# Moving a bias table forward, joining value products, and moving half of a modulation: a two-block transformer kernel on one core

## The chip, the cores and the metric

The kernel runs on 1 core of one Trainium2 chip. The metric is the device time of one execution in microseconds (us); the median of 3 runs before the change is 2052.93 us (2050.81 to 2061.72). Names of engines: PE is the matmul engine, PEld its weight loads, DVE the vector engine, ACT the scalar engine, POOL the GpSimd engine, SP the engine that issues most loads. ACTq and SPq are DMA issues by ACT and by SP.

## The reference, cut to what matters

Two transformer blocks run one after the other on 512 tokens of width 1024, in float32. The first block mixes by two kinds of attention with a relative-position bias, then has a SwiGLU feed-forward. The second block has two layers whose normed input is scaled and shifted by vectors ("modulation") computed from one conditioning vector `c`:

```python
# first block
xn = rms_norm(h, norm1_g); aq, ak, av, ... = split_columns(xn @ w_in)
o_a = mixer_dilated(aq, ak, av, rel_bias[:, :8])     # 8 heads, bias of the distance
o_b = gates over compressed, selected and window attention (8 heads, rel_bias[:, 8:])
h = h + concat(o_a, o_b) @ w_out
h = h + (silu(hn @ w_gate) * (hn @ w_up)) @ w_down   # hn = rms_norm(h), 2816 hidden
x = rms_norm(h, norm_f_g)
# second block, layers i = 0 (gated linear attention + attention), 1 (window attention)
mod_l = split(silu(c) @ mod_w[i] + mod_b[i], 6)      # mod_w[i]: 1024 x 6144
h_l = rms_norm_2(x, norm_mix[i]) * (1 + mod_l[1]) + mod_l[0]
x = x + mod_l[2] * mixer(h_l);  x = x + mod_l[5] * hier_moe(modulated x)
```

`mod_w[i]` does not depend on the tokens, so the modulation vectors of both layers can be computed at any time ahead of their use. Layer 1's are first needed in layer 1, at the end of layer 0's expert part.

## The kernel before, in words

**Arithmetic.** Every float32 product is made of three matmuls of split operands (high times high, low times high, high times low): lines L155, L156, L157. A weight tile of 128x1024 (512 KB, one load by SP) is cast to its high half on ACT (`whi`, L149) and subtracted for its low half on DVE (`wlo`, L150). In `even_layer`, `proj_T` takes POOL for that subtraction when three projections share one pass (`eng=nc.gpsimd`).

**Order.** A scheduler puts all instructions in one order per engine when the program is built, and each engine runs its list in that order, waiting on semaphores. DMAs are issued by an engine's queue, so they stand in these lists too.

**Bias table.** `first_block` makes a table of biases. After the value projection `w_av`, `bias_rows()` loads three small tables by ACT, multiplies them (L302), finishes them on DVE (L303), stores the result `bd` (16x640) and copies every row of it 128 times to a table `bf` of [16, 128, 640] in memory (5.24 MB): four DMAs of 1280 KB each, issued by ACT. `bias_tile` later loads, for each head and half of the queries, one tile `wb` of 128 rows out of `bf`, each row one element further on: 32 loads by SP (L131). DVE subtracts `wb` from the scores (L384).

**Attention.** Scores go through a softmax on DVE and ACT (`sc`), four PE transposes (`tr`, L199), an eviction to `pt`, and the value products `po` (L404 in the first block, L2166 in the last layer; values `av`, `bvn`, `avN`, `ovN`). `Fill` hands PE work from the head before while a head's scores are made: one call between two groups of scores issues `n` items, here FILL0, FILL1 and FILLA = 1.

**Modulation.** `mod_steps` (L692) is a generator; one step loads 128 rows of `mod_w` (512 KB, SP) for 1024 of the columns and adds `row * silu(c)` to a 128x1024 accumulator `macc` by two DVE instructions (L709 for the first, L711 for the rest). After eight steps PE sums the partitions (L718), and the row is added to `modrow` (L721). 16 steps and a tail make one third (`rd`), three thirds a layer. Layer 0's 48 steps are spread over the first block's feed-forward by `next(steps, None)`. Layer 1's 48 steps are spread over `even_layer`, one after each projection piece and after each output of the linear attention; what is left is done before `m_es.close()`.

**Operand of layer 0.** `cross_norm` (L960 to L971) norms the feed-forward's result; `modulated_T` transposes it (L199 `tr<-ident,X`), scales it on ACT to `ms` (L769), and DVE makes the halves `ahi`, `alo` (L771, L772). Then come the projections of layer 0, the gates `gG` of the linear attention, its scans (L1096, L1098), states and outputs (`gat` L1161, `go` L1165, `sr` L1172).

Of the kernel before, what the change touches and what calls it, by code (L numbers as in the profile page):

```python
# [19 lines left out]
P = 128  # L20
# [44 lines left out]
FILL0 = 1  # L65
FILL1 = 1
# [5 lines left out]
FILLA = 1  # L72
# [143 lines left out]
def first_block(K, st, h_es):  # L216

    tc, nc, io, small = K.tc, K.nc, K.io, K.small
    es = ExitStack()
    g1 = K.c.tile([P, KT], F32, name="g1")  # L220
# [8 lines left out]
    def acc():  # L229
        return ps_a.tile([P, 512], F32, name="acc", tag="acc", bufs=2)  # L230

    xn = K.act_lat()
    with ExitStack() as w_es:
        work = K.pool(w_es, "b1w")
        x = work.tile([P, NT, D], F32, name="x")
        for t in range(NT):
            K.load(x[:, t], io["x"][t * P:(t + 1) * P])
        for p in range(2):
            xs = []
            for t in (2 * p, 2 * p + 1):  # L240
                junk = work.tile([P, D], BF16, name="junk", tag="junk", bufs=2)
                r = K.rsqrt(K.sumsq(x[:, t], junk), D)
                nc.vector.tensor_scalar(x[:, t], x[:, t], r, None, op0=OP.mult)
                xs.append(x[:, t])
            normed_T(K, ps_t, xs, 2, g1, lambda k: (xn[0][:, k, 256 * p:256 * p + 256], xn[1][:, k, 256 * p:256 * p + 256]))

# [42 lines left out]


    bd = K.dram.tile([16, 640], F32, name="bd")
    bf = K.dram.tile([16, P, 640], F32, name="bf")

    def bias_rows():
        t1, t2, bv = [att.tile([P, 1024], F32, name="bt", tag="pt", bufs=4) for _ in range(3)]
        relb, oneh, brow, bv = t1[:32, 640:656], t1[:32, :640], t2[:16, :640], bv[:16, :640]
        K.store(relb, io["rel_bias"])
        K.store(oneh, io["c_onehot"])
        K.store(brow, io["c_brow"])
        for s0, w in ((0, 512), (512, 128)):  # L300
            ps = acc()
            nc.tensor.matmul(ps[:16, :w], relb, oneh[:, s0:s0 + w], start=True, stop=True)  # L302
            nc.vector.scalar_tensor_tensor(bv[:, s0:s0 + w], ps[:16, :w], -1.0, brow[:, s0:s0 + w],  # L303
                                           op0=OP.mult, op1=OP.subtract)
        K.store(bd, bv)
        for h in range(0, 16, 4):
            K.store(bf[h:h + 4], bd[h:h + 4, None, :].to_broadcast([4, P, 640]))
# [212 lines left out]
    bias_rows()  # L520
# [73 lines left out]
    steps = mod_steps(K, st, 0, st["pool"], ps_t)  # L594
    def ff_up(f):
        pss = []
        for i, src in enumerate((io["w_gate"], io["w_up"])):
# [9 lines left out]
            next(steps, None)  # L607
# [20 lines left out]
    for f in range(22):  # L628
        ff_up(f)
        if f == CTX_AT:  # L630
            for _ in steps:
                pass
# [7 lines left out]
        if f == parts[0][1]:  # L640

            f0, f1 = parts.pop(0)
            for ch in range(2):
                chunks = load(f0, f1, ch)
                for t in range(NT):
# [3 lines left out]
                    if t:  # L649
                        next(steps, None)  # L650
# [19 lines left out]
    for t in range(NT):  # L670
# [7 lines left out]
        if t % 2:  # L678
            modulated_T(K, work, ps_t, xs, gs, cols, 0, h, P * (t - 1))
# [12 lines left out]
def mod_steps(K, st, l, pool, psum):  # L692
# [4 lines left out]
    for rd in range(3):  # L697
# [190 lines left out]
class Fill:  # L888


    def __init__(self, n):
        self.n, self.todo = n, iter(())

    def __call__(self):
        for _ in range(self.n):
# [80 lines left out]
def even_layer(K, st, h, rt):  # L976
# [20 lines left out]
    steps = mod_steps(K, st, 1, modp, ps_t)  # L997
# [4 lines left out]
    def proj_T(parts, *pairs):  # L1002
        ws = [K.weights(io["ev_s"][i], eng=nc.gpsimd if len(pairs) == 3 else None) for i, _ in pairs]
        for sl in parts:
            for w, (_, evac) in zip(ws, pairs):
# [4 lines left out]
                next(steps, None)  # L1010

    def proj_N(src, width, evac, parts=((4, 5, 0, 1, 2, 3),)):
        chunks = [K.weights(src[kp]) for kp in range(KT * width // D)]
        for ts in parts:
            for t in ts:
# [3 lines left out]
                next(steps, None)  # L1019
# [129 lines left out]
    def outputs(j):  # L1149
        ss = small.tile([P, CH, 2], F32, name="gss", tag="gss", bufs=2)  # L1150
        s4 = sr.rearrange("p c (h d) -> p c h d", h=4)
        for ch in (4, 5, 1, 2, 0, 3):
            cs = slice(ch * P, (ch + 1) * P)
            for e in range(2):
# [18 lines left out]
                next(steps, None)  # L1173
# [1188 lines left out]
def body(nc, tc, io, out, stop=None, skip1=False, force_slow=False):  # L2362
    with ExitStack() as es:
# [9 lines left out]
        if skip1:  # L2373
# [3 lines left out]
            with ExitStack() as mes:  # L2377
# [9 lines left out]
                for p in range(3):  # L2387
# [5 lines left out]
                    modulated_T(K, work, pt, xs, gs, cols, p // 2, h, 256 * p)  # L2393
# [86 lines left out]
```

## Time and profile before

| what | value |
|---|---|
| median of 3 runs (lowest, highest) | 2052.93 us (2050.81, 2061.72) |
| profiled execution, its own time | 2055.75 us |
| its span | 2054.0 us |
| PE busy | 1814.8 us, 88% of the span |
| DVE busy | 1456.9 us, 71% |
| ACT busy | 934.6 us, 46% |
| POOL busy | 421.2 us, 21% |
| mean granted clock of PE | 0.934 |
| DMA moved | 314.80 MB, mean 153 GB/s |

The span is the time from the first to the last instruction of the profiled execution; its own time is 1.75 us longer, and 2.82 us above the median of the runs. Busy time is an average over stages with different limits. A timeline row gives the start in us, the duration in us, engine, line, operation, output and inputs and, in brackets, how long the engine was idle before it and what it waited for. A row of a table by stretch gives the stretch, its length, the busy time of PE, PEld, DVE, ACT and POOL in it (instructions in parentheses), the granted clock as a share of the full one, the busy share of the DMA engines and the GB/s moved.

### The profile page before, as it was taken

What the parts mean: (1) busy time and instruction counts of PE and PEld (TensorE: products, weight loads), DVE (VectorE), ACT (ScalarE), POOL (GpSimd) and SP (SyncE); (2) the same over time, 40 slices, a digit from 0 to 9 for tenths busy, and PEclk for the clock granted to TensorE, in tenths of its full rate; (3) what the DMA queues carried; (4) which work ended last, traced back from release to release, by engine and by line L of the source; (5) the groups of instructions that cost most, each with busy time, mean ns of one, the idle gap of its engine ahead of it and who ended that gap; (6) DMA issues with size and microseconds to landing.
All of it is one profiled execution on the core that took longest, in us unless ns stands there. A gap on an engine that the chain in (4) does not pass through costs nothing. (4 is left out here: it accounts for less than half of the span.)

```text
span 2054.0 us, 27111 instructions
## 1 busy us (share of the span) xinstructions
PE 1814.8 (88%) x9494; PEld 1368.3 (67%) x9494; DVE 1456.9 (71%) x2809; ACT 934.6 (46%) x1777; POOL 421.2 (21%) x330
## 2 busy tenths in 40 slices
PE   7499999899999996898978998599957899978997
PEld 5377865777777775676756677476746666765664
DVE  4264676697676448667867635799979877568999
ACT  4264465422222233421325732378844467426673
POOL 0010011100000011030222122333234411144752
PEclk9799999999999997897989999699978999988998
DMA  6333221475655225454430144489852100548983
GB/s 220 137 100 104 83 62 52 138 242 167 199 174 173 81 88 161 144 157 160 154 101 1 42 176 154 170 313 348 304 201 85 42 1 12 200 157 275 329 288 137
DMA packets 99662, 314.80 MB, mean 153 GB/s; under 512 B 15904, under 2 KB 19617, under 8 KB 99505
## 3 DMA queue, kind: packets, MB, share of 16 engines
q1 hardware_dynamic: 77856, 267.97, 39.3%
q10 hardware_dynamic: 13168, 23.91, 3.1%
q0 software_dynamic: 8480, 20.98, 3.0%
q8 instruction: 78, 1.28, 0.3%
q14 instruction: 80, 0.65, 0.1%
HBM read 291.18 MB, written 36.32 MB: 159 GB/s over the span
## 5 line engine op out<-in xcount | busy, mean ns | idle before, releaser
L149 ACT CAST whi<-wraw 128x1024 fp32r<-128x1024 f32 (+1 forms) x345 | 359.1, 1045 | 417.7 <-PE acc L156 134.3
L150 DVE TENSOR_TENSOR wlo<-wraw,whi 128x1024 fp32r<-128x1024 f32 (+1 forms) x337 | 400.9, 1214 | 93.2 <-ACT whi L149 89.8
L711 DVE SCALAR_TENSOR_TENSOR macc<-wraw,silu,macc 128x1024 f32<-128x1024 f32 x168 | 214.8, 1317 | 12.7 <-DMA wraw<-mod_w 12.7
L155 PE MATMUL acc<-ahi,whi 128*128 128x512 f32 (+1 forms) x576 | 215.5, 375 | 3.6 <-ACT whi L149 1.7
L157 PE MATMUL acc<-ahi,wlo 128*128 128x512 f32 (+1 forms) x576 | 215.0, 374 | 3.7 <-DVE wlo L150 3.7
L156 PE MATMUL acc<-alo,whi 128*128 128x512 f32 (+1 forms) x576 | 215.1, 374 | 0.0
L199 PE MATMUL tr<-ident,sc 128*128 128x128 f32 x752 | 128.8, 287 | 2.2 <-DVE alo L213 0.7
L155 PEld LDWEIGHTS acc<-ahi,whi 128*128 128x128 f32 x576 | 109.4, 190 | 26.3 <-ACT fhi L161 2.5
L157 PEld LDWEIGHTS acc<-ahi,wlo 128*128 128x128 f32 x576 | 109.8, 191 | 22.4 <-DVE wlo L150 4.1
L199 PEld LDWEIGHTS tr<-ident,sc 128*128 128x128 f32 x752 | 82.0, 141 | 63.3 <-issue 34.3
L156 PEld LDWEIGHTS acc<-alo,whi 128*128 128x128 f32 x576 | 109.7, 190 | 18.7 <-issue 0.4
L156 PE MATMUL gu<-wlo,xhi 128*128 128x512 f32 (+1 forms) x264 | 110.1, 417 | 12.1 <-DVE wlo L150 10.8
L155 PE MATMUL acc<-whi,ahi 128*128 128x512 f32 (+2 forms) x288 | 105.9, 372 | 8.1 <-DVEq L1227 8.1
L157 PE MATMUL gu<-whi,xlo 128*128 128x512 f32 (+1 forms) x264 | 106.0, 401 | 2.7 <-DVE xlo L161 2.6
L155 PE MATMUL gu<-whi,xhi 128*128 128x512 f32 (+1 forms) x264 | 106.9, 405 | 0.9 <-ACT xhi L161 0.8
L157 PE MATMUL acc<-whi,alo 128*128 128x512 f32 (+2 forms) x288 | 104.8, 368 | 1.0 <-DVE alo L772 1.0
L156 PE MATMUL acc<-wlo,ahi 128*128 128x512 f32 (+2 forms) x288 | 104.7, 366 | 0.8 <-DVE wlo L150 0.8
L1733 POOL DMA_INDIRECT xg<-hD,xidx x33 | 72.5, 2197 | 149.2 <-PE yo L157 64.4
L928 POOL COPY rw<-rd 128x256 f32<-128x256 f32 x52 | 21.5, 413 | 363.0 <-DVE rd L934 165.5
L1743 POOL DMA_INDIRECT yD<-y,idx x33 | 73.1, 2217 | 87.8 <-DVE y L1813 29.1
L962 POOL TENSOR_TENSOR xs<-X,gf 128x1024 f32<-128x1024 f32 x2 | 5.8, 2922 | 367.5 <-DVE X L622 367.5
L884 PE MATMUL sps<-Kh,Q 128*128 128x256 f32 (+2 forms) x208 | 73.6, 361 | 7.1 <-DVE mn L2140 5.5
(548 smaller groups left out, 4402.9 us busy)
## 6 DMA issues: line engine op xcount, KB each, us to landing
wraw<-ew SPq DMA_DIRECT2D x198, 512.0 KB
wraw<-mod_w SPq DMA_DIRECT2D x96, 512.0 KB
wraw<-w_gate SPq DMA_DIRECT2D x22, 512.0 KB
wraw<-w_up SPq DMA_DIRECT2D x22, 512.0 KB
wraw<-w_down SPq DMA_DIRECT2D x22, 512.0 KB
wraw<-yD SPq DMA_DIRECT2D x20, 512.0 KB
wraw<-w_s SPq DMA_DIRECT2D x16, 512.0 KB
wraw<-w_out SPq DMA_DIRECT2D x12, 512.0 KB
```

What stands on the lines that cost most here:

```text
L149: nc.scalar.copy(hi[:, :n], raw[:, :n])
L150: (eng or nc.vector).tensor_tensor(lo[:, :n], raw[:, :n], hi[:, :n].bitcast(F32), op=OP.subtract)
L155: mm(out, a[0], b[0], start=start, stop=False)
L156: mm(out, a[0], b[1], start=False, stop=False)
L157: mm(out, a[1], b[0], start=False, stop=stop)
L199: self.nc.tensor.transpose(out, src, self.ident[:n, :n])
L711: nc.vector.scalar_tensor_tensor(acc[:, r], w, sr, acc[:, r], op0=OP.mult, op1=OP.add)
L884: K.nc.tensor.matmul(ps, q, Kh[:, cols], start=True, stop=False)
L928: K.nc.gpsimd.tensor_copy(rw, r[:, :, :, None].to_broadcast([P, 2, 2, 64]))
L962: (V if late else nc.gpsimd).tensor_tensor(y, x, gf, op=OP.mult)
L1733: return nc.gpsimd.indirect_dma_start(out=xg[:c], out_offset=None, in_=mo["hD"], bounds_check=n * P - 1, oob_is_err=False, in_offset=bass. ...
L1743: sc = nc.gpsimd.indirect_dma_start(out=yD.rearrange("t k d -> (t k) d"), out_offset=bass.IndirectOffsetOnAxis(ap=idx[:c, b:b + 1].bitcast ...
```

## The change

Four things change.

- The three small tables are loaded first of all by ACT, the two matmuls and two DVE instructions on them stand at the program's start, and `bd` and `bf` are written by POOL's queue behind the norm of `x`. `bf` has 32 copies of each row instead of 128 (1.31 MB, two DMAs), and each `wb` tile is loaded in four DMAs of 32 rows.
- `Fill` issues on every second call only, three items instead of one (FILL0, FILL1), or two (FILLA).
- `mod_steps` takes the thirds to do. Layer 1's first third follows layer 0's steps in the feed-forward's calls, what is left of it is done behind the loop, and its two other thirds stay in `even_layer`, each step ordered behind the last instruction of layer 0's operand (`tc.issue_after`).
- `proj_T` of `even_layer` always subtracts on DVE.

```diff
-FILL0 = 1
-FILL1 = 1
+FILL0 = 3
+FILL1 = 3
-FILLA = 1
+FILLA = 2
...
+    K.store(relb, io["rel_bias"])
+    K.store(oneh, io["c_onehot"])
+    K.store(brow, io["c_brow"])
     g1 = K.c.tile([P, KT], F32, name="g1")
...
+    bf = K.dram.tile([16, 32, 640], F32, name="bf")
+    for s0, w in ((0, 512), (512, 128)):
+        ps = acc()
+        nc.tensor.matmul(ps[:16, :w], relb, oneh[:, s0:s0 + w], start=True, stop=True)
+        nc.vector.scalar_tensor_tensor(bv[:, s0:s0 + w], ps[:16, :w], -1.0, brow[:, s0:s0 + w],
+                                       op0=OP.mult, op1=OP.subtract)
...
+    nc.gpsimd.dma_start(bd, bv)
+    for h in range(0, 16, 8):
+        nc.gpsimd.dma_start(bf[h:h + 8], bd[h:h + 8, None, :].to_broadcast([8, 32, 640]))
...
-        K.store(bd, bv)
-        for h in range(0, 16, 4):
-            K.store(bf[h:h + 4], bd[h:h + 4, None, :].to_broadcast([4, P, 640]))
...
-        src = bass.AP(tensor=bf.tensor, offset=bf.offset + h * P * 640 + 127 + (2 - 2 * p) * P, ap=[[639, P], [1, n]])
-        K.load(w[:, :n], src)
+        for r in range(0, P, 32):
+            src = bass.AP(tensor=bf.tensor, offset=bf.offset + h * 32 * 640 + 127 + (2 - 2 * p) * P - r, ap=[[639, 32], [1, n]])
+            K.load(w[r:r + 32, :n], src)
...
     proj_N(io["w_av"], 512, lambda t, ps: nc.any.tensor_copy(av[:, t], ps))
-    bias_rows()
...
-    steps = mod_steps(K, st, 0, st["pool"], ps_t)
+    mods = [mod_steps(K, st, 0, st["pool"], ps_t), mod_steps(K, st, 1, st["pool"], ps_t, (0,))]
+
+    def step():
+        while mods and next(mods[0], 1):
+            mods.pop(0)
...
+    while mods:
+        step()
     m_es.close()
...
         if t % 2:
-            modulated_T(K, work, ps_t, xs, gs, cols, 0, h, P * (t - 1))
+            st["mark"] = modulated_T(K, work, ps_t, xs, gs, cols, 0, h, P * (t - 1)).ins
...
-        for _ in range(self.n):
+        self.calls += 1
+        for _ in range(0 if self.calls % 2 else self.n):
             next(self.todo, None)
...
-    steps = mod_steps(K, st, 1, modp, ps_t)
+    steps = mod_steps(K, st, 1, modp, ps_t, (1, 2))
+
+    def step():
+
+        with tc.issue_after(st["mark"]):
+            next(steps, None)
...
-        ws = [K.weights(io["ev_s"][i], eng=nc.gpsimd if len(pairs) == 3 else None) for i, _ in pairs]
+        ws = [K.weights(io["ev_s"][i]) for i, _ in pairs]
```

What the scheduler makes of it is seen at three places. A row is a number, the line, the operation, output and inputs, the output's size and, with x, how many stand in a row; lines of the changed kernel are those of its own file.

DVE at the program's start, before:

```order
7 L180 TENSOR_SCALAR ss<-ss 128x1
8 L243 TENSOR_SCALAR x<-x,rs 128x1024
9 L180 TENSOR_SCALAR ss<-ss 128x1
10 L243 TENSOR_SCALAR x<-x,rs 128x1024
11 L213 SCALAR_TENSOR_TENSOR alo<-tr,g_83,ahi 128x256 x2
12 L150 TENSOR_TENSOR wlo<-wraw,whi 128x1024 x2
```

and now:

```order
5 L245 SCALAR_TENSOR_TENSOR bv<-acc,brow 16x512
6 L245 SCALAR_TENSOR_TENSOR bv<-acc,brow 16x128
7 L180 TENSOR_SCALAR ss<-ss 128x1 x4
8 L150 TENSOR_TENSOR wlo<-wraw,whi 128x1024 x3
9 L259 TENSOR_SCALAR x<-x,rs 128x1024 x4
10 L213 SCALAR_TENSOR_TENSOR alo<-tr,g_93,ahi 128x256 x2
```

The bias rows `bv` and three low halves of `w_av` now stand ahead of the scaling of `x`.

PE in the last layer's attention, before:

```order
6803 L2166 MATMUL po<-pt,ovN 64x256 x2
6804 L199 MATMUL tr<-ident,sc 128x128 x5
6805 L884 MATMUL sps<-Kh,Q 128x256
6806 L885 MATMUL sps<-Kl,Q 128x256
6807 L884 MATMUL sps<-Kh,Q 128x256
6808 L885 MATMUL sps<-Kl,Q 128x256
6809 L2166 MATMUL po<-pt,ovN 64x256 x2
```

and now:

```order
6758 L199 MATMUL tr<-ident,sc 128x128 x4
6759 L893 MATMUL sps<-Kh,Q 128x384
6760 L894 MATMUL sps<-Kl,Q 128x384
6761 L893 MATMUL sps<-Kh,Q 128x256
6762 L894 MATMUL sps<-Kl,Q 128x256
6763 L2182 MATMUL po<-pt,ovN 64x256 x4
6764 L2182 MATMUL po<-pt,ovN 64x128 x2
```

The same 416 value products of the four attentions stand in 106 uninterrupted runs instead of 199 (`av` 18 instead of 21, `bvn` 28 instead of 47, `avN` 25 instead of 53, `ovN` 35 instead of 78).

DVE behind the operand of layer 0, before:

```order
743 L711 SCALAR_TENSOR_TENSOR macc<-wraw,silu,macc 128x1024
744 L772 TENSOR_TENSOR alo<-ms,ahi 128x256
745 L771 CAST ahi<-ms 128x256
746 L711 SCALAR_TENSOR_TENSOR macc<-wraw,silu,macc 128x1024
747 L772 TENSOR_TENSOR alo<-ms,ahi 128x256
748 L771 CAST ahi<-ms 128x256
```

and now:

```order
748 L781 TENSOR_TENSOR alo<-ms,ahi 128x256
749 L804 TENSOR_TENSOR evqc<-cos,evqg 128x256
750 L805 TENSOR_TENSOR evqs<-sin,evqg 128x256
751 L804 TENSOR_TENSOR evkc<-cos,evkg 128x256
752 L805 TENSOR_TENSOR evks<-sin,evkg 128x256
753 L718 TENSOR_SCALAR macc<-wraw,silu 128x1024 x2
754 L720 SCALAR_TENSOR_TENSOR macc<-wraw,silu,macc 128x1024 x14
755 L150 TENSOR_TENSOR wlo<-wraw,whi 128x1024 x3
756 L730 TENSOR_TENSOR modrow<-modrow,tr 64x512
757 L718 TENSOR_SCALAR macc<-wraw,silu 128x1024 x2
758 L720 SCALAR_TENSOR_TENSOR macc<-wraw,silu,macc 128x1024
759 L1103 COPY gkT<-acc 128x256
```

The steps of the modulation no longer stand between the halves of the operand but in one block behind them, ahead of the gates, which begin two rows further on.

## Rows read from the trace of the kernel before

**Rows 1.** Busy time by stretch (columns as said above).

```profile
50.00:100.00 50.00, 21.18 (x82) 16.92 (x80) 9.10 (x11) 7.65 (x12) 0.00 (x0) 0.69 0.38 138
...
105.00:361.00 256.00, 247.19 (x1426) 180.44 (x1425) 159.53 (x445) 142.12 (x355) 26.16 (x48) 1.00 0.27 78
...
650.00:750.00 100.00, 100.00 (x443) 79.63 (x442) 38.51 (x57) 26.95 (x35) 0.00 (x0) 1.00 0.27 81
...
850.00:926.00 76.00, 76.00 (x351) 57.71 (x350) 51.45 (x65) 25.45 (x44) 15.95 (x15) 0.98 0.44 145
...
967.00:1047.00 80.00, 71.11 (x465) 56.82 (x465) 66.35 (x99) 27.24 (x79) 16.66 (x12) 0.91 0.51 158
...
1640.00:1810.00 170.00, 163.12 (x1054) 117.25 (x1052) 115.81 (x290) 100.05 (x255) 29.65 (x42) 0.97 0.21 80
```

**Rows 2.** Timeline of PE around its long gap.

```profile
56.48 0.39 PE L157 MATMUL acc<-ahi,wlo 128*128 128x512 f32 x1
84.63 0.47 PE L884 MATMUL sps<-akh,aq 128*128 128x128 f32 x1 [27.76 <-ACT akh L878]
86.16 0.77 PE L155 MATMUL acc<-ahi,whi 128*128 128x512 f32 x1 [1.06 <-DVE aq L867]
...
91.84 0.53 PE L156 MATMUL acc<-alo,whi 128*128 128x512 f32 x1
```

**Rows 3.** Timeline of ACT's queue in the same stretch.

```profile
50.09 32.79 ACTq L134 DMA_DIRECT2D bf<-bd  x4
```

**Rows 4.** Four microseconds in which only the table is written (columns of rows 1).

```profile
74.00:78.00 4.00, 0.00 (x0) 0.00 (x0) 0.00 (x0) 0.00 (x0) 0.00 (x0) 0.50 0.26 104
```

**Rows 5.** Timeline at the start, of ACT and of PE.

```profile
17.95 1.98 ACT L149 CAST whi<-wraw 128x1024 fp32r<-128x1024 f32 x2
...
16.33 0.78 PE L155 MATMUL acc<-whi,ahi 128*128 128x512 f32 x1
```

**Rows 6.** Timeline of SP: two loads of bias tiles back to back.

```profile
104.12 0.80 SPq L131 DMA_DIRECT2D wb<-bf  x2
```

**Rows 7.** Timeline of PE: value products in runs of 4 and of 14.

```profile
1704.10 0.65 PE L2166 MATMUL po<-pt,ovN 128*64 128x256 f32 x4
1704.68 0.77 PE L199 MATMUL tr<-ident,sc 128*128 128x128 f32 x5
...
1705.64 0.28 PE L885 MATMUL sps<-Kl,Q 128*128 128x256 f32 x1
1705.85 0.65 PE L2166 MATMUL po<-pt,ovN 128*64 128x256 f32 x4
...
164.28 1.73 PE L404 MATMUL po<-pt,av 128*64 128x256 f32 x14
165.94 0.44 PE L199 MATMUL po<-ident,rw 128*128 128x128 f32 x2
```

**Rows 8.** Timeline of DVE and of POOL from the operand of layer 0 to the gates.

```profile
763.62 0.75 DVE L970 TENSOR_SCALAR X<-xs,rs 128x1024 f32<-128x1024 f32 x1 [2.90 <-POOL rs L185]
...
778.89 2.83 DVE L970 TENSOR_SCALAR X<-xs,rs 128x1024 f32<-128x1024 f32 x1 [0.59 <-POOL rs L185]
...
782.84 1.27 DVE L711 SCALAR_TENSOR_TENSOR macc<-wraw,silu,macc 128x1024 f32<-128x1024 f32 x1
...
808.00 0.42 DVE L772 TENSOR_TENSOR alo<-ms,ahi 128x256 fp32r<-128x256 f32 x1
...
836.85 0.48 DVE L1064 TENSOR_SCALAR gG<-acc,gb 128x256 f32<-128x256 f32 x1
...
778.83 2.34 POOL L150 TENSOR_TENSOR wlo<-wraw,whi 128x1024 fp32r<-128x1024 f32 x1
```

**Rows 9.** Timeline of DVE at the second scan of the linear attention.

```profile
972.84 9.65 DVE L711 SCALAR_TENSOR_TENSOR macc<-wraw,silu,macc 128x1024 f32<-128x1024 f32 x8
982.41 1.75 DVE L1096 TENSOR_TENSOR_SCAN gG<-rmask,gG 128x768 f32<-128x768 f32 x1
```

**Rows 10.** Groups of instructions by line, DVE, 967 to 1047 us.

```profile
L711 DVE SCALAR_TENSOR_TENSOR macc<-wraw,silu,macc 128x1024 f32<-128x1024 f32 x28 | 34.6, 1277 | 0.0
```

More of the change, by code (lines that the diff above doesn't have):

```diff
@@ L219, in first_block @@
     es = ExitStack()
+    rows_es = ExitStack()
+    tables = K.pool(rows_es, "b1r", side="right")
+    relb, oneh, brow, bv = [tables.tile([m, w], F32, name=nm) for m, w, nm in
+                            ((32, 16, "relb"), (32, 640, "oneh"), (16, 640, "brow"), (16, 640, "bv"))]
+    K.store(relb, io["rel_bias"])
+    K.store(oneh, io["c_onehot"])
+    K.store(brow, io["c_brow"])
     g1 = K.c.tile([P, KT], F32, name="g1")
@@ L230, in acc @@
         return ps_a.tile([P, 512], F32, name="acc", tag="acc", bufs=2)
+    bd = K.dram.tile([16, 640], F32, name="bd")
+    bf = K.dram.tile([16, 32, 640], F32, name="bf")
[4 more added lines that the diff above has]
+                                       op0=OP.mult, op1=OP.subtract)
     xn = K.act_lat()
@@ L245, in first_block @@
             normed_T(K, ps_t, xs, 2, g1, lambda k: (xn[0][:, k, 256 * p:256 * p + 256], xn[1][:, k, 256 * p:256 * p + 256]))
+    nc.gpsimd.dma_start(bd, bv)
+    for h in range(0, 16, 8):
+        nc.gpsimd.dma_start(bf[h:h + 8], bd[h:h + 8, None, :].to_broadcast([8, 32, 640]))
+    rows_es.close()
     ps_s = K.pool(ps_es, "b1s", PSUM, bufs=2)
@@ L288, in keys @@
         return kk
[L291 to L304, printed above, removed]
-        K.store(bd, bv)
-        for h in range(0, 16, 4):
-            K.store(bf[h:h + 4], bd[h:h + 4, None, :].to_broadcast([4, P, 640]))
     posT = proj.tile([P, 16], F32, name="posT")
@@ L606, in ff_up @@
             pss.append(ps)
-            next(steps, None)
+            step()
         sg = ffn.tile([P, S], F32, name="sg", tag="sg", bufs=2)
@@ L630, in first_block @@
         if f == CTX_AT:
-            for _ in steps:
-                pass
+            while len(mods) > 1:
+                step()
             xs = []
@@ L649, in first_block @@
                     if t:
-                        next(steps, None)
+                        step()
+    while mods:
+        step()
     m_es.close()
@@ L689, in mod_state, with mod_steps @@
             "cols": [K.c.tile([P, 48, 2], F32, name="cols%d" % l) for l in range(2)]}
-def mod_steps(K, st, l, pool, psum):
+def mod_steps(K, st, l, pool, psum, thirds=range(3)):
     nc, io = K.nc, K.io
     cols = st["cols"][l]
-    for rd in range(3):
+    for rd in thirds:
         rows = pool.tile([P, 512], F32, name="modrow", tag="modrow", bufs=1)
@@ L891, in __init__ @@
     def __init__(self, n):
-        self.n, self.todo = n, iter(())
+        self.n, self.calls, self.todo = n, 0, iter(())
     def __call__(self):
-        for _ in range(self.n):
+        self.calls += 1
+        for _ in range(0 if self.calls % 2 else self.n):
             next(self.todo, None)
@@ L1009, in proj_T @@
                 evac(sl, ps[:, :n])
-                next(steps, None)
+                step()
     def proj_N(src, width, evac, parts=((4, 5, 0, 1, 2, 3),)):
@@ L1018, in proj_N @@
                 evac(t, ps[:, :width])
-                next(steps, None)
+                step()
             yield
@@ L1172, in outputs @@
                 nc.vector.tensor_tensor(s1, o, s1, op=OP.mult)
-                next(steps, None)
+                step()
         rs = K.rsqrt(ss.rearrange("p c e -> p (c e)"), P).rearrange("p (c e) -> p c e", e=2)
@@ L2392, in body @@
                         xs.append(normed(K, work, y, y))
-                    modulated_T(K, work, pt, xs, gs, cols, p // 2, h, 256 * p)
+                    st["mark"] = modulated_T(K, work, pt, xs, gs, cols, p // 2, h, 256 * p).ins
+                for _ in mod_steps(K, st, 1, st["pool"], pt, (0,)):
+                    pass
         else:
```

## The prediction

> **What bounds the kernel now.** I read the busy time by stretch first, then the timelines where PE is not full, since PE is busy 88% of the span. In the feed-forward and in the projections of layer 0 PE is full (100.00 of 100, 76.00 of 76), and in the two attentions nearly so (247.19 of 256, 163.12 of 170) [rows 1]; there only less PE work, or fewer losses between PE's instructions, can gain. Three stretches are different. From 50 to 100 us PE works 21.18 of 50 us. In layer 0's operand, from 750 us on, PE waits for DVE's halves. From 967 to 1047 us DVE is busy for 66.35 of 80 us, and PE's 71.11 are at a granted clock of 0.91 [rows 1]: neither is full, and they wait for each other.
>
> **1. The bias table.** PE ends its projection at 56.48 + 0.39 = 56.87 us and waits 27.76 us, and 1.06 more at 86.16 [rows 2]. The name on the wait is an ACT cast, but ACT's own list says why it was late: the four DMAs of the table hold ACT at their issue from 50.09 for 32.79 us, to 82.88 [rows 3]. After the pause PE is at the lower of its clocks (1.2 instead of 2.4 GHz, granted 0.50 at 74 to 78 us [rows 4]): 13 matmuls go from 86.16 to 91.84, 0.437 us each [rows 2], where 443 take 100 us at full clock, 0.226 each [rows 1]. That is 13 x 0.21 = 2.7. With nothing behind that issue the gain is 27.8 + 1.1 + 2.7 = 31.6; I take **-31** (bounds -29 to -32).
>
> What covers the new place: the table must be there before the first scores need it, which before were made at about 100 us, and would be at 100 - 31 + 3 = 72. It is now 1.31 MB instead of 5.24, and 104 GB/s is the pace at which the old one was written with nothing beside it [rows 4]: 12.6 us. Begun at some 15 us behind the norm's four small POOL operations, it would end near 30 and leave about 40 us. If that cover went, each us of it would be lost.
>
> A rule weighs against POOL's queue. [Rows 8] show DVE's scaling of `X` taking 2.83 us while POOL subtracts (778.83 + 2.34 = 781.17), against 0.75 us alone: the two block each other. The Trainium skill, "SBUF — State Buffer", section "SBUF: two separate sides", explains such blocking by one shared port pair, and says that POOL writes the descriptors of its own DMAs and is kept from it by some DVE operations, where ACT's and SP's queues are not. The first half agrees with the 2.83; for the DMA no run here shows it, and by it the table would come some DVE operations later. It is a part of rival C.
>
> **2. The start.** DVE does three `wlo` ahead of scaling `x`, where `x` came first. The third cast of `w_av` began at 17.95 (two in 1.98, so 1 us each) [rows 5]; with 1.2 for its `wlo`, scaling of 0.75 [rows 8], transposes and a high half of some 1 us, the first product matmul comes at 17.95 + 1.0 + 1.2 + 0.75 + 1 = 21.9 at the latest rather than 16.33 [rows 5]; a weight that is cast as it lands may save 1. So +4.5 to +5.5. The two bias matmuls leave their old place on PE, with some 1.8 us there. Net **+3** (bounds 0 to +8, if the tables land late and hold DVE's first instructions).
>
> **3. Bias tiles in quarters.** 96 more loads. Two issues back to back take 0.80 us [rows 6], 0.40 each, so 38 us of SP more in the 256 us of the first attention and what follows [rows 1]; SP waits for free buffers most of that time. **0** (bound 0 to +5).
>
> **4. Value products in runs.** PE changes the kind of work at both ends of a run. In the long run 14 products go from 164.28 to 165.94, 0.119 each [rows 7]. The run of 4 at 1704.10 should release PE at 1704.57, but the transposes start at 1704.68: 0.11 lost. A score matmul of this size takes as long as a value product, 0.12, so the one at 1705.64 should release it at 1705.76, and the products start at 1705.85: 0.09 lost. So 0.2 us a run, and 199 - 106 = 93 runs go: 18. It counts in full only where PE is the bound; by the busy shares of 96% and 97% it is for most of the time [rows 1]. I take **-15** (bounds -18 to 0: the softmax's DVE and ACT chain could take the place).
>
> **5. The operand.** Between 782.84 and 808.00 DVE does ten modulation instructions of 1.27 among the last halves of the operand, and POOL blocks two scalings for 2.83 - 0.75 = 2.1 each [rows 8]: 12.7 + 4.2 = 17 that go. But they come again: 16 instructions, 1.21 each where several stand in a row [rows 9], 19 us, now stand in one block ahead of the gates, which started at 836.85 [rows 8]. Of the 17 I let **-10** reach the gates, as PE has projections of its own to do in that block; behind the gates it is full again (76.00 of 76 from 850 [rows 1]), so what is gained stays. Bounds -17 to 0.
>
> **6. The last third.** The scan at 982.41 stood behind eight modulation instructions in a row, 9.65 us [rows 9]. In 967 to 1047 there are 28 of them, 34.6 us [rows 10], and without them DVE has 66.35 - 34.6 = 32 us of 80. PE then sets the pace: 71.11 x 0.91 = 64.7 us at full clock [rows 1], 15 less than 80; as busy times of short groups of matmuls overlap, somewhat less than that. I take **-18** (bounds -8, the scan's wait alone, to -31).
>
> **7. The feed-forward.** It gets 16 steps: 32 instructions of some 1.28 us, 41 us [rows 10], and 8.4 MB. From 650 to 750 DVE is busy 38.51 of 100 and the DMA engines 27% [rows 1], so 61 us are free and the block fits; PE stays the bound. What isn't covered is the tail behind the loop, some transposes and copies: **+2** (bounds 0 to +6; were all of it exposed, +41).
>
> **The sum.** 3 - 31 + 0 - 15 - 10 - 18 + 2 = **-69**. The profiled execution took 2055.75 us, so 1986.75; it lies 2.8 above the median of the runs, 2052.93, so I forecast **1984 us**.
>
> **The rivals.**
> A. The modulation is only moved (20%). Its 32 remaining steps take as long on DVE, and ahead of the gates they hold them as long as before; the last third gives only the scan's wait. Then 5 is 0 and 6 is -8: -49, so 2004. For it: DVE is busy 51.45 of 76 us in the projections [rows 1]; against it, that DVE had room there all along.
> B. The runs give nothing (12%), as longer waits between the groups let DVE and ACT set the pace: 4 is 0, -54, so 1999. For it: DVE 115.81 and ACT 100.05 of 170 us [rows 1] are in one chain; against it, PE is idle for only 8.8 and 6.9 us there [rows 1].
> C. The table comes late (5%), half of the pause stays: -54, 1999. It decides from some 40 us of delay on.
> D. Slower, by SP (3%). The quarters wait for each other: 128 loads over the 256 us of [rows 1] leave 2.0 us each. If one held the queue for 2.6 us, 128 would take 333 us, 77 more than there are, and the gain of 69 would be gone: 2060. The 0.40 us of [rows 6] speaks against it. The Trainium skill, "DMA: Bandwidth & Descriptors", section "Anatomy of one DMA", gives about 2.0 us of fixed time to each DMA and, under "Bandwidth", wants 1 MiB a transfer, so it speaks against the quarters; by it, 128 x 2.0 = 256 us would just fit if they ran one behind the other. That pair shows that the next is issued well inside such a time.
> E. The tail of the feed-forward is exposed (4%): 2 becomes 41, so 2023.
> Better than forecast (6%): 5 and 6 at their far ends, -17 and -31, give -89, so 1964.
>
> **How the numbers follow.** The forecast has 50%. With every gain at its far end, 0 - 32 - 18 - 17 - 31 + 0 = -98, the time is 1955; the upper end is A with some of B and E, 2016. The range 1955 to 2016 leaves out most of D and E, and the mixtures of A with B, 2 in 10 or less. A measurement here can tell about 0.5% from no change, 10 us, so faster means under 2042.7 and slower over 2063.2. All but D, and the far end of E, are faster: 0.94; the same 0.03; slower 0.03.
>
> **What the profile should show.** PE's gap at 57 us gone, with ACT free of long issues; `bf` written before 40 us; the first product matmul near 21; about 93 fewer ends of `po` runs, and both attentions shorter (together by about 15); no modulation instruction between the halves of layer 0's operand, which ends some 17 us sooner after the feed-forward, but gates only 10 sooner; no `macc` among the linear attention's second outputs, and that stretch about 18 shorter. The prediction is wrong if PE shows a new wait of over 10 us, on `wb`, on `mod_w` or behind the feed-forward, or if the attentions do not get shorter.

## The result and the profile after

| | median, us | runs | lowest to highest |
|---|---|---|---|
| before | 2054.69 | 4 | 2050.81 to 2061.72 |
| changed | 1974.05 | 4 | 1972.22 to 1976.77 |

The ratio is 0.9605, with a 95% interval of 0.9575 to 0.9635: 80.6 us less, where 69 less was forecast; the time lies in the range (1955 to 2016). The span of the profiled execution fell from 2054.0 to 1974.2 us.

The stretches of the changed kernel, in the columns of [rows 1]. They answer to them in order, but their bounds are those of this kernel's stages, so that shares can be held against each other and lengths cannot: the old place of the pause, the first block from the dilated attention's last score to the feed-forward's first addition, the end of the feed-forward, the projections of layer 0, the linear attention, the last attention.

```profile
50.00:100.00 50.00, 48.13 (x242) 36.84 (x241) 29.09 (x64) 30.91 (x71) 2.66 (x5) 1.00 0.43 129
130.00:439.00 309.00, 294.70 (x1684) 232.76 (x1683) 198.17 (x431) 147.12 (x324) 25.36 (x47) 0.98 0.38 118
650.00:744.00 94.00, 91.49 (x406) 70.77 (x404) 66.13 (x97) 29.61 (x43) 6.16 (x4) 1.00 0.46 144
789.00:884.00 95.00, 86.85 (x366) 61.57 (x366) 72.64 (x88) 34.84 (x61) 15.96 (x15) 0.89 0.55 178
884.00:974.00 90.00, 83.62 (x517) 64.76 (x517) 56.86 (x110) 26.14 (x83) 10.44 (x12) 0.89 0.34 111
1582.40:1692.20 109.80, 109.48 (x850) 84.53 (x850) 84.95 (x245) 85.57 (x230) 19.10 (x34) 1.00 0.07 21
```

From 50 to 100 us PE now works 48.13 of 50 us instead of 21.18 [rows 1]. The start, on PE:

```profile
17.00 1.43 PE L199 MATMUL tr<-ident,x 128*128 128x128 f32 x4 [7.15 <-DVE x L259]
18.78 0.80 PE L155 MATMUL acc<-whi,ahi 128*128 128x512 f32 x1 [0.35 <-ACT ahi L212]
```

and on POOL, whose queue writes the table:

```profile
10.65 0.69 POOL L263 DMA_DIRECT2D bd<-bv  x1 [10.20 <-DVE ss L180]
11.45 3.96 POOL L185 TENSOR_TENSOR rs<-ss,half 128x1 f32<-128x1 f32 x4
15.96 1.98 POOL L265 DMA_DIRECT2D bf<-bd  x2 [0.55 <-DMA bd<-bv]
```

The first product comes at 18.78 us, 2.5 later than before [rows 5], and the table's two DMAs are issued at 16 and 17 us. The trace has them landing 11.9 and 13.7 us after their issue, so by some 31 us. SP's first load of a bias tile is issued at 49.76, and DVE first uses one at 63.67.

A run of value products in the last attention, which answers to [rows 7]: 12 rows of products in one run where there were 4 (the trace has two rows for each product of the program, 832 for the 416), and scores that go straight over into transposes.

```profile
1591.39 0.28 PE L894 MATMUL sps<-Kl,Q 128*128 128x256 f32 x1
1591.60 1.30 PE L2182 MATMUL po<-pt,ovN 128*64 128x256 f32 x12
1592.83 0.66 PE L199 MATMUL tr<-ident,sc 128*128 128x128 f32 x4
...
1593.80 0.28 PE L894 MATMUL sps<-Kl,Q 128*128 128x256 f32 x1
1593.91 0.27 PE L199 MATMUL tr<-ident,sc 128*128 128x128 f32 x1
```

DVE in layer 0's operand and at the scan, which answers to [rows 8, 9]: the scaling takes 0.75 us and the halves of the operand end at 761.8; then come the 16 modulation instructions in a block of 18 us, and the scan has none ahead of it.

```profile
750.55 0.75 DVE L980 TENSOR_SCALAR X<-xs,rs 128x1024 f32<-128x1024 f32 x1 [0.59 <-POOL rs L185]
...
761.35 0.43 DVE L781 TENSOR_TENSOR alo<-ms,ahi 128x256 fp32r<-128x256 f32 x1
...
765.10 1.41 DVE L718 TENSOR_SCALAR macc<-wraw,silu 128x1024 f32<-128x1024 f32 x2
766.42 16.82 DVE L720 SCALAR_TENSOR_TENSOR macc<-wraw,silu,macc 128x1024 f32<-128x1024 f32 x14
...
927.66 1.83 DVE L1193 TENSOR_TENSOR sr<-sr,rs 128x768 f32<-128x768 f32 x2 [2.19 <-POOL rs L185]
929.40 1.75 DVE L1112 TENSOR_TENSOR_SCAN gG<-rmask,gG 128x768 f32<-128x768 f32 x1
```

**Where the 80 us came from.** The view of one tile gives the start of the first and of the last instruction of a group; such starts cut the program into ten stages. Here the line for the linear attention's score matmuls in the changed kernel, first at 884.2 and last at 974.2 us:

```profile
L1175 PE MATMUL ga<-gqf,gG x48: 272/272/418, 884.2 to 974.2; 64*128 64x128 f32 x48
```

Length of each stage in us, for the two kernels and for the first four experiments (each has parts of the change, see below; "no runs" is the changed kernel with the old `Fill`, "mod. undone" the changed kernel with the old modulation):

| stage, from the end of the one above | before | changed | runs only | table only | no runs | mod. undone |
|---|---|---|---|---|---|---|
| start to the dilated attention's last score | 159.9 | 129.6 | 158.3 | 131.0 | 129.7 | 128.7 |
| to the feed-forward's first addition | 311.9 | 309.1 | 317.0 | 313.1 | 316.8 | 307.9 |
| to its last addition | 303.1 | 305.0 | 302.3 | 303.1 | 305.0 | 302.2 |
| to the linear attention's first score | 151.1 | 140.5 | 150.4 | 151.9 | 139.2 | 150.5 |
| to its last score | 116.2 | 90.0 | 116.0 | 116.0 | 90.5 | 115.9 |
| to the transpose of its output | 54.9 | 60.2 | 54.2 | 55.1 | 60.1 | 54.9 |
| to layer 0's last value product | 108.3 | 99.0 | 99.2 | 108.3 | 108.2 | 99.1 |
| to layer 1's first value product | 449.5 | 449.0 | 449.6 | 450.2 | 450.9 | 449.2 |
| to its last value product | 118.6 | 109.8 | 109.7 | 118.6 | 118.7 | 110.1 |
| to the last product out of an expert's hidden units (`yo`) | 257.0 | 257.9 | 255.8 | 257.3 | 254.6 | 256.0 |

The differences of the second column to the first are -30.3, -2.8, +1.9, -10.6, -26.2, +5.3, -9.3, -0.5, -8.8 and +0.9, -80.4 together. The second stage, here called the first block's second attention, also holds that attention's projections and the start of the feed-forward.

### The profile page after: what moved, and what is told of

The parts are those of the page before. It is cut to its first block, busy times and chain, and to the rows that moved or that the text cites. A ratio compares the mean times of both kernels' runs of the same rounds, so it can differ in the third digit from the quotient of the medians.

```text
span 1974.2 us, 27271 instructions
## 1 busy us (share of the span) xinstructions
PE 1781.0 (90%) x9494; PEld 1368.3 (69%) x9494; DVE 1441.9 (73%) x2792; ACT 939.2 (48%) x1797; POOL 410.8 (21%) x330
## 5 line engine op out<-in xcount | busy, mean ns | idle before, releaser
L150 DVE TENSOR_TENSOR wlo<-wraw,whi 128x1024 fp32r<-128x1024 f32 (+1 forms) x340 | 405.0, 1213 | 96.9 <-ACT whi L149 90.8
L156 PEld LDWEIGHTS acc<-alo,whi 128*128 128x128 f32 x576 | 109.6, 190 | 18.5 <-issue 0.4
```

The lines of the kernel that those rows point to most:

```text
L150: (eng or nc.vector).tensor_tensor(lo[:, :n], raw[:, :n], hi[:, :n].bitcast(F32), op=OP.subtract)
L156: mm(out, a[0], b[1], start=False, stop=False)
```

## Experiments

The times stand against the kernel before on the same chip (2056.5 to 2057.3 us median); the changed kernel itself was timed on another, against 2054.7, so differences of 2 or 3 us to it say nothing.

### One part alone, one part undone

`runs_only`: the kernel before with the new `Fill`.

```diff
-FILL0 = 1
-FILL1 = 1
+FILL0 = 3
+FILL1 = 3
...
-FILLA = 1
+FILLA = 2
...
-        for _ in range(self.n):
+        self.calls += 1
+        for _ in range(0 if self.calls % 2 else self.n):
```

> The kernel before with the change of Fill alone (three items, or two, on every second call; the table and the modulation as before). Theory 'ends of runs': PE loses 0.2 us for each run of value products that goes, and nothing else changes: 93 runs, 15 to 18 us, so 2037 to 2040 where the kernel before takes 2054.7. Theory 'more than ends': the changed kernel's trace shows 3.8 us less in the first block's attention, some 9 to 10 in layer 0's and 8.8 in layer 1's, 22 together, because the longer groups also spare PE waits for the softmax: 2033. Rival 'softmax chain': ACT and DVE set the pace, so nothing: 2052 to 2056.

`no_runs`: the same lines undone in the changed kernel.

> The changed kernel with the Fill of before (one item on each call). Theory 'ends of runs': 15 to 18 us more than the changed kernel's 1974: 1989 to 1992. Theory 'more than ends': 22 more, 1996. If the parts of the change add up, the loss here is the gain of the kernel that has the runs alone; if it is smaller, part of that gain stood in waits that the modulation's move takes away too.

`table_only`: the kernel before with the early table, 32 copies and quarter loads.

> The kernel before with the bias table alone (early table on POOL's queue, 32 copies, quarter loads of the bias tiles; Fill and the modulation as before). Theory 'the pause goes, the start costs 2 to 3': 29 to 30 us less than before, 2025. Rival 'the quarters cost': SP's 96 further issues delay weights or bias tiles, so that less than 24 is gained, 2031 or more. Rival 'the start costs as much as forecast at its bound, 8': 2031 as well, but then the first product matmul stands at 24 us or later.

`mod_undone`: the changed kernel with the modulation and the POOL subtractions of before.

```diff
-    mods = [mod_steps(K, st, 0, ...), mod_steps(K, st, 1, ..., (0,))]
...
+    steps = mod_steps(K, st, 0, st["pool"], ps_t)
...
-    steps = mod_steps(K, st, 1, modp, ps_t, (1, 2))
+    steps = mod_steps(K, st, 1, modp, ps_t)
...
-        with tc.issue_after(st["mark"]):
-            next(steps, None)
+        next(steps, None)
...
-        ws = [K.weights(io["ev_s"][i]) for i, _ in pairs]
+        ws = [K.weights(io["ev_s"][i], eng=nc.gpsimd if len(pairs) == 3 else None) for i, _ in pairs]
```

> The changed kernel with layer 1's modulation as before (all 48 steps in layer 0's mixer, not ordered behind the operand, low halves of three weights on POOL). Theory by stretches of the two traces: operand to gates 10.6, last third 21, less 2 for the feed-forward's longer end, so about 29 more than 1974: 2003. Rival 'only moved' (the modulation costs as much in its new place): 10 or less more, 1984. If the three parts add up, this is 2054.7 less the gains of the other two kernels that have one part each.

| kernel | median, us | ratio to before, 95% interval |
|---|---|---|
| runs only | 2039.25 | 0.9915, 0.9882 to 0.9949 |
| table only | 2027.24 | 0.9853, 0.9811 to 0.9896 |
| no runs | 2000.50 | 0.9729, 0.9694 to 0.9765 |
| modulation undone | 2006.58 | 0.9766, 0.9728 to 0.9804 |

**The table** gives 2056.5 - 2027.2 = 29 us, as the first theory said. The interval (21 to 39 us) would leave room for the rivals' 24, but the trace does not: the first stage is 28.9 us shorter (159.9 to 131.0), and the first product matmul stands at 19.53 us, where a rival wanted 24 or later. The quarters and the start together took no more than the forecast had left them.

**The modulation** undone costs 2006.6 - 1974.05 = 32.5, expected 29. The stages of the profiled executions say where: 10.0 between the feed-forward and the linear attention, 25.9 in it, less 2.8 in the feed-forward and 5.3 behind the linear attention. These are 27.8 together; the profiled execution with the modulation undone took 2000.64 us, 6 less than the median, so its stages show less than the medians do. This kernel has the other two parts of the change, and 2054.7 less their gains, 29 and 17, is 2008: there the parts add up.

**The runs** alone give 17 us, which is the number of the theory 'ends of runs', but by luck; undone they cost 26 us, which is more than the other theory's 22. The stages show why. Layer 0's and layer 1's attentions gain 9.1 and 8.9 us in one kernel and 9.2 and 8.9 in the other. The first block's second attention differs: the runs make it 7.7 us shorter with the early table (316.8 to 309.1), and 5.1 longer without it (311.9 to 317.0). Three windows of that stage in `runs_only`, in the columns of [rows 1], and the one of the kernel before that answers to the second:

```profile
210.50:218.50 8.00, 8.00 (x67) 7.91 (x65) 4.60 (x9) 5.28 (x10) 0.00 (x0) 1.00 0.18 61
218.50:226.50 8.00, 8.00 (x37) 7.25 (x37) 5.41 (x20) 0.83 (x2) 0.00 (x0) 0.61 0.63 201
...
326.50:342.50 16.00, 13.95 (x66) 8.75 (x65) 8.99 (x21) 8.39 (x21) 2.33 (x3) 0.68 0.33 98
```

```profile
220.00:228.00 8.00, 8.00 (x50) 6.95 (x50) 6.20 (x24) 1.11 (x3) 0.00 (x0) 1.00 0.58 191
```

PE is busy without a gap and its granted clock falls from 1.00 to 0.61 all the same, where the kernel before keeps 1.00; from 326 us on it is 0.68. In windows of 4 us over this stage, the missing share of the clock adds up to 15.3 us in `runs_only`, 1.7 in the kernel before, 6.8 in the changed one and 8.5 in `no_runs`. Taken as lost time, which is an estimate, these sums leave 310.2 - 301.7 = 8.5 us that the runs save beside the old table and 308.3 - 302.3 = 6.0 beside the new one. The other kernels bear the estimate out: five more with the runs and the new table (`mod_undone`, `pool_split`, `no_mark`, `third_back`, `act_queue`) take 306.0 to 310.9 us in this stage with 3.4 to 8.6 missing, which leaves 302.3 to 303.0 in each; `table_only`, without the runs, is left with 308.0. So the runs shorten all three attentions in both kernels, and the kernel that has them alone gives some 14 us back to the clock.

### The modulation's move taken apart

`pool_split`: `eng=nc.gpsimd if len(pairs) == 3 else None` back in the changed kernel's `proj_T`.

> The changed kernel with the low halves of three weights on POOL again. Theory 'POOL and DVE block each other': two scalings of the operand take 2.1 us longer each, so the operand ends some 4 us later and 1976 to 1979 us. Rival 'DVE is full there anyway': the 3 x 1.2 us that DVE saves make up for it, 1973 to 1975. The rows to read are those of the scaling (0.75 or 2.8 us).

`no_mark`: the steps in `even_layer` without their order.

```diff
-        with tc.issue_after(st["mark"]):
-            next(steps, None)
+        next(steps, None)
```

> The changed kernel without the order behind the operand: the 16 modulation instructions of the next third may stand between the halves of layer 0's operand again. Theory of the prediction (what goes from the operand comes again ahead of the gates, and 10 of 17 us stay): 7 to 10 us more, 1981 to 1984. Rival 'only moved': gates start no later than now, 1974. The row to read is the first gate matmul, 788.9 us in the changed kernel.

`third_back`: layer 1's first third back in `even_layer`.

```diff
-    mods = [mod_steps(K, st, 0, ...), mod_steps(K, st, 1, ..., (0,))]
+    mods = [mod_steps(K, st, 0, st["pool"], ps_t)]
...
-    steps = mod_steps(K, st, 1, modp, ps_t, (1, 2))
+    steps = mod_steps(K, st, 1, modp, ps_t)
```

> The changed kernel with layer 1's first third back in layer 0's mixer, all 48 steps behind the operand. Theory 'last third': the scan and the second outputs wait for 32 more modulation instructions, 21 us, and the feed-forward's end is 2 to 3 us sooner: 1991 to 1993. Rival 'feed-forward pays': the 16 steps cost the feed-forward as much as they cost the mixer, 1974 to 1978.

| kernel | median, us | interval of the ratio | operand, after the feed-forward | to the first gate matmul | to the first linear score | first to last score |
|---|---|---|---|---|---|---|
| before | 2054.69 | | 32.8 | 25.8 | 92.5 | 116.2 |
| changed | 1974.05 | 0.9575 to 0.9635 | 18.6 | 26.6 | 95.3 | 90.0 |
| pool_split | 1977.44 | 0.9588 to 0.9631 | 22.5 | 24.7 | 95.4 | 90.9 |
| no_mark | 1977.38 | 0.9594 to 0.9663 | 25.4 | 25.5 | 89.8 | 90.8 |
| third_back | 1994.43 | 0.9678 to 0.9726 | 19.0 | 26.0 | 94.9 | 115.9 |
| mod_undone | 2006.58 | 0.9728 to 0.9804 | 32.7 | 24.7 | 93.1 | 115.9 |

(The last four columns are us of the profiled execution, cut at DVE's first rope table, `evqc`, and at the first gate matmul. With the order the rope table starts behind the operand's last half; without it, it stands 0.8 us (before, `mod_undone`) or 1.6 us (`no_mark`) ahead of the end of that half.)

`third_back` is the theory 'last third': 20 us more, with 25.9 more in the linear attention, 5.0 less behind it and 3.0 less in the feed-forward (302.0 instead of 305.0). Moving those 16 steps is what shortened the scan and the second outputs.

`pool_split` shows the blocking again, but not in the rows that the expectation named: both scalings take 0.75 us, and while POOL makes its halves, three instructions on DVE's halves take 2.1 to 2.6 us, among them one `alo` with 2.47 instead of 0.42.

```profile
757.29 2.47 DVE L781 TENSOR_TENSOR alo<-ms,ahi 128x256 fp32r<-128x256 f32 x1
```

```profile
754.75 4.73 POOL L150 TENSOR_TENSOR wlo<-wraw,whi 128x1024 fp32r<-128x1024 f32 x2 [5.20 <-ACT whi L149]
```

The operand is 3.9 us longer, as its theory says, and 1.9 of it is back by the first gate; the medians, 3 us apart, can't be told apart. `no_mark` has the modulation between the halves again, its operand is 6.8 us longer and its gates begin 5 us later, as the forecast's theory says, but the first linear score is where it was (883.6 and 884.2). PE's waits changed their place with it. The longest of PE's waits in this stretch, in total, times, and the longest, first in `no_mark`, at the operand, and then in the changed kernel, at the gates:

```profile
PE tr L199 <- ACT ms L778: 8.1, 7, 1.8
```

```profile
PE acc L1077 <- DVE gkT L1103: 5.1, 1, 5.1
```

So with the order, or with all subtractions on DVE, or with both, the way from the feed-forward to the linear attention takes 140 to 143 us; only with neither it takes 151. (`mod_undone`, the kernel with neither, also has the first third's steps there; with the order they cost nothing on this way, 139.9 us in `third_back`.) On this way PE is idle for 24.2 us at a mean clock of 0.85 in the kernel before and for 22.4 at 0.85 in `mod_undone`, but for 17.1 at 0.89 in the changed kernel and for 15.3 at 0.88 in `no_mark`: the gain is shorter waits and a higher clock. One more thing goes with it. DVE's waits for `mod_w` in this stretch, in total, times, and the longest, first with modulation undone and then in the changed kernel:

```profile
DVE macc L714 <- DMA wraw<-mod_w: 13.4, 4, 3.9
```

```profile
DVE macc L720 <- DMA wraw<-mod_w: 1.3, 1, 1.3
```

The kernel without the order has no such wait at all. Whether the late loads of `mod_w` are the cause, or follow from the later operand, no run here separates.

### The table's size and queue

`one_wb`: 128 copies of each row and one load for each bias tile, in the changed kernel.

```diff
-    bf = K.dram.tile([16, 32, 640], F32, name="bf")
+    bf = K.dram.tile([16, P, 640], F32, name="bf")
...
-        for r in range(0, P, 32):
...
+        K.load(w[:, :n], src)
```

> The changed kernel with 128 copies of each bias row (5.24 MB, still two DMAs on POOL's queue) and one load for each bias tile. Theory 'queue' (the pause came from ACT standing at its issues, and quarters cost nothing): the table is written from 16 us on at 104 GB/s or more, so it lands at 66 us at the latest where it is first used at 63.7, and the time is 1974 to 1984. Rival 'volume' (the 5.24 MB delay the weights too): 20 us or more back, 1994 or more. Rival 'the quarters cost': faster than 1974 by the 96 issues that go, if the table is in time.

`act_queue`: the early table of 1.31 MB by ACT's queue.

```diff
-    nc.gpsimd.dma_start(bd, bv)
+    K.store(bd, bv)
...
-        nc.gpsimd.dma_start(bf[h:h + 8], ...)
+        K.store(bf[h:h + 8], ...)
```

> The changed kernel with the early table written by ACT's queue instead of POOL's (same 1.31 MB in two DMAs). Theory 'ACT stands at its issues until the transfer has nearly passed': the second DMA's issue lasts 5 to 12 us at about 20 us, the operand's high halves on ACT wait for it and the first product matmuls too: 1979 to 1986. Rival 'small tables pass': two DMAs of 640 KB are taken at once, ACT's issues last 1 us each, 1973 to 1976; then the place and the size took the pause away, and POOL's queue did nothing.

`act_queue` takes 1972.98 us (0.9594, 0.9541 to 0.9647): nothing lost. ACT's two issues, to be held against [rows 3]:

```profile
18.22 1.23 ACTq L134 DMA_DIRECT2D bf<-bd  x1
21.21 0.90 ACT L212 ACTIVATE ahi<-tr,g 128x256 fp32r<-128x256 f32 x2 [2.58 <-PE tr L199]
21.65 0.65 ACTq L134 DMA_DIRECT2D bf<-bd  x1
```

They hold ACT for 1.23 and 0.65 us, not for 32.79. So the pause did not go because POOL's queue took the table, but because the table became small and early. Whether size or place did more on ACT's queue was not tried apart; on POOL's queue even the large table's two issues took only 1.43 and 1.15 us (`one_wb`).

`one_wb` takes 1990.15 us (0.9674, 0.9651 to 0.9698): 16 us lost, and not by any of the three theories. The table was in time: both its DMAs landed 25.9 us after their issue, by some 43 us. In 24 to 40 us the DMA engines carry 371 GB/s (last column):

```profile
24.00:40.00 16.00, 16.00 (x80) 12.14 (x79) 6.26 (x14) 6.10 (x13) 0.00 (x0) 1.00 1.02 371
```

but SP's list has another order. The scheduler put ten weight loads ahead of the first bias tile, and the first eight tiles are loaded from 89.02 us on, where the changed kernel loads its first four, as 16 quarters, from 49.76:

```profile
49.88 39.08 SPq L142 DMA_DIRECT2D wraw<-w_s  x10
89.02 11.14 SPq L131 DMA_DIRECT2D wb<-bf  x8
```

and DVE waits for the tile (4.05 us at 92.66), with PE behind it. So the smaller table and its quarter loads, which this run undid together, paid by letting the bias tiles into SP's order early. What the 96 further issues cost by themselves stays open, since the order changed with them.

### Further along the same way

`runs_longer`: `Fill` on every fourth call, six items (FILLA four).

> The changed kernel with Fill on every fourth call only (six items, or four): 70 runs of value products instead of 106. Theory 'ends of runs' with the 26 us that 93 runs were worth in the changed kernel, 0.28 each: 36 x 0.28 = 10 less, 1964. Rival 'softmax chain': the products come so late that scores and their evictions wait, PE shows waits on DVE or ACT in the attentions, and the time is 1974 or more.

1977.03 us (0.9613, 0.9560 to 0.9667): not faster, though 36 more runs went. Layer 1's attention is 2.3 us shorter (107.5), layer 0's 1.3 longer (81.2 instead of 79.9 from first to last value product), in the first block PE waits 2.4 us for ACT's high half of the attention's output (0.4 in the changed kernel), and the clock lacks 12.0 us in the first block's second attention instead of 6.8, where kernels with the changed one's runs lacked 3.4 to 8.6. The theory 'ends of runs', which promised 10 us, is refuted for longer runs; the rival's waits are there but small, and a part of what was won may have gone to the clock.

`ff_two`: two of layer 1's thirds in the feed-forward.

```diff
-    mods = [..., mod_steps(K, st, 1, st["pool"], ps_t, (0,))]
+    mods = [..., mod_steps(K, st, 1, st["pool"], ps_t, (0, 1))]
...
-            step()
+            for _ in range(1 + i):
+                step()
...
-    steps = mod_steps(K, st, 1, modp, ps_t, (1, 2))
+    steps = mod_steps(K, st, 1, modp, ps_t, (2,))
```

> The changed kernel with two of layer 1's thirds in the feed-forward (a second step at every up projection), one third left in layer 0's mixer. Theory 'what leaves the mixer is gained while PE covers it': the block ahead of the gates and the first outputs lose 32 modulation instructions, 41 us of DVE, of which a quarter to a half was on the path as with the last third: 8 to 16 less, 1958 to 1966. Rival 'the cover is used up': DVE is busy 36 to 42 of each 50 us in the feed-forward already, and with 41 us more PE waits there for halves of weights: 5 to 20 more than that, so 1970 to 1985.

`ff_two_later`: with `range(1 + (i and f > 2))`.

> As the kernel with two thirds in the feed-forward, but the second step at an up projection only from the fourth hidden tile on, when the first weights of the feed-forward are through. Theory 'the cover was used up only at the start' (there PE waited 4.2 us for a high half and lost 1.8 more at the lower clock): 4 to 6 us less than that kernel's 1967, so 1961 to 1963, and 11 to 13 less than the changed kernel. Rival 'the whole feed-forward is short of DVE': the loss only moves, 1966 to 1970.

They take 1967.38 (0.9562, 0.9508 to 0.9617) and 1965.32 us (0.9559, 0.9534 to 0.9584), each between the ranges of its theory and its rival. The linear attention of the second, to be held against the changed kernel's 90.0 us:

```profile
890.00:962.00 72.00, 69.45 (x502) 56.31 (x501) 36.17 (x86) 23.98 (x82) 11.59 (x12) 1.00 0.21 70
```

It takes 71.5 us instead of 90.0, with PE nearly full and the clock at 1.00 instead of 0.89. Of these 18.5 us some 7.5 are not gained: the feed-forward's first addition comes 5.2 us later and it is 2.3 us longer in `ff_two_later`. In `ff_two` it was 5.4 and 4.0. PE's wait of 4.2 us at the start of the feed-forward is gone with the later second step, yet the first addition is no earlier. But the expectation is not refuted by this: ahead of 345 us, before the first step of the modulation, where PE and DVE still do the same in both, the clock lacks 6.8 us in `ff_two_later` and 1.7 in `ff_two`, and these 5 us are about what the wait was worth. The two versions can't be told apart by their times, so whether the start alone was short of cover stays open. All five runs of the last one (1957.83 to 1968.22) lie below all four of the changed kernel, 8.7 us by the medians, though on another chip.

## Why the prediction was right

**1. and 2., the table and the start: -28 forecast, -29 measured.** The reading of [rows 3], that ACT stood at its issues, was right in its size. The first product came 2.5 us later, where 4.5 to 5.5 were forecast with 1.8 of it to come back; in its net, the 31.6 of the pause less the 28.9 (`table_only`) to 30.3 found, the start cost 1 to 3. What POOL's queue was credited with, it did not do: ACT's queue takes the small table just as well. Rival C, and with it the Trainium skill's page "SBUF — State Buffer", section "SBUF: two separate sides", on POOL's descriptors being held up, found no place to show: the table was in memory by some 31 us, 19 us ahead of its first load.

**3., quarter loads: 0 forecast.** Nothing in the first stage contradicts it (table only: 131.0), and rival D, that the quarters wait for each other, did not come: 16 of them were issued from 49.76 to 58.84 us, 0.57 us each. The some 2 us of fixed time that the Trainium skill's page "DMA: Bandwidth & Descriptors" states in "Anatomy of one DMA", there for the DMAs that GpSimd issues, did not become SP's time. That the 96 further issues cost nothing by themselves is not shown, as `one_wb` changed the order with them.

**4., the runs: -15 forecast, -26 measured (no_runs against changed).** This is the term that was mis-sized. The step "0.2 us a run" held for layer 1's attention: 43 runs, 8.8 us, 0.2 each. Layer 0's gave 9.2 for 28, 0.33 each, and the first block's 6.0 to 7.7 for the other 22 (`av` 3, `bvn` 19). Counting each PE instruction from its start to the next one's, between the first and the last value product, the products take 6.3 us less in layer 0's and 4.9 in layer 1's, the transposes 1.9 and 3.1 less and the scores 1.0 and 0.8. The transposes and scores are not cut into fewer pieces for it: in layer 0's attention they stand in 47 and 41 groups before and in 46 and 38 now, in layer 1's in 65 and 63 before and in 67 and 61 now. That what they save lies at their borders to the products, as the forecast had it, is likely but not shown. Why a run was dearer in layer 0's attention stays open. And the cut from 18 to 15 for the softmax chain was for nothing in the last attention: PE stayed the bound (109.48 of 109.80 us).

**5., the operand: -10 forecast, -10.6 found, which was luck.** The operand did end sooner after the feed-forward, by 14.2 us up to the rope table and by 15.4 up to the end of its last half (17 forecast), and the gates came nearer by 13.4, more than the 10 forecast. Nothing waited for the block ahead of them: PE's first gate matmul waits 1.1 us, and for ACT. What was lost again, 2.8 us up to the linear score, goes with the wait of 5.1 us for `gkT`, ahead of which DVE has the next steps of the modulation. And the share that lasted does not hang on the block: with the modulation between the halves again (`no_mark`) the linear attention starts no later. That either the order or DVE's subtractions alone would bring it, the forecast, which added up the two, did not have. Its reading of [rows 8] missed one of the blocked instructions: of the ten modulation instructions one took 3.38 us beside POOL.

**6., the last third: -18 forecast, -20.9 found.** It is 26.2 less in the linear attention and 5.3 more behind it, where matmuls of a projection that had run among the second outputs now follow them: between the last score and the output's transpose there are 54 of each of its three forms instead of 32, 66 more, while the wait behind them is 2.6 us shorter. `third_back` shows the mechanism.

**7., the feed-forward: +2 forecast, +1.9 found** (3.0 against `third_back`).

The sum was off by 12 us in the end. By the stages of the two kernels the three attentions with runs give 20.9 us where 15 was forecast, the last third 2.9 and the first stage 2.3 more than forecast. The 26 us of the runs come down to these 20.9 in the first block's second attention, which without the runs takes 316.8 us in the changed kernel and took 311.9 before; the clock lacks 8.5 us there instead of 1.7. The forecast had no term for the clock in that stage.

## What to carry to other kernels

When an engine issues DMAs between its computations, read its own list, and not the name on the wait: the issues of a large transfer can hold the engine, here for 32.79 us. Work that must be done at some time is cheapest where another engine is full and its own is not; watch for what the other engine's stage pays, which here grew with the second third. Price gathering from more than one place, as a run was worth 0.2 us in one attention and 0.33 in another, and take a gain read from one execution together with its clock, for a part tried alone can lose at the clock what it wins in PE's order.

## What the runs showed of the hardware

The granted clock fell in stretches in which PE was full: from 1.00 to 0.61 between two neighbouring windows of 8.00 busy of 8 us (`runs_only`, above), while the kernel before had 1.00 at the same work. Over the executions of a kernel this repeats: all four of `runs_only` have a mean clock of 0.926 to 0.929, where six of the seven of the kernel before on the same chip have 0.933 to 0.935 and one has 0.929. What makes it fall there stays open. And the four DMAs of the old table moved 104 GB/s with nothing beside them [rows 4], where the same 5.24 MB landed within some 27 us by POOL's queue among weight loads (`one_wb`, some 190 GB/s by this estimate, with 371 GB/s on all DMA engines together): the old pace was no limit of the table's.
